# A hybrid mLSTM/GLA decoder block: the first two units side by side, with halved weight loads, constant products at the start and three squares on GpSimd

## The chip, the core and the metric

The kernel runs on one core of a Trainium2 chip. The core has a matrix engine (TensorE, PE in the profile), a vector engine (VectorE, DVE), an activation engine (ScalarE, ACT), a general engine (GpSimd, POOL) and a queue engine that issues DMAs (SyncE, SP). The engines run side by side, each takes its own instructions strictly in order, and they wait for each other by semaphores. The metric is the device time of one execution in microseconds (us); lower is better. Matmul results go to eight PSUM banks; everything else lies in SBUF.

## What is computed

The block takes 512 tokens of width 1024 and 16 learned meta tokens ahead of them, 528 in all. The part that matters here is its first step: a root-mean-square norm, and one wide projection of its result.

```python
def rmsnorm(x, g):
    xf = x.astype(jnp.float32)
    y = xf * lax.rsqrt(jnp.mean(xf * xf, axis=-1, keepdims=True) + EPS)
    return (y * g.astype(jnp.float32)).astype(x.dtype)
...
        xn = rmsnorm(h, norm1_g[l])
        proj = jnp.where(valid, xn @ w_in[l].astype(dt), 0.0).astype(dt)
        (mq, mk, mv, mi, mf, mo, gq, gk, gv, ga, gr, gate_m, gate_g) = split_cols(proj)
```

The columns of `proj` feed two token mixers (an mLSTM and a gated linear attention, both by chunks), whose results are merged by gates, projected and added to the input; a second norm and a SwiGLU follow, and a last norm. All of it is in float32.

## The kernel before

*Units.* All weights are cut into slices of 128 output columns. A slice is one unit: a tile of 128 partitions by 1024, whose eight blocks of 128 columns belong to the eight tiles of x. x lies transposed, as eight tiles `xs[k]` of 128 features by 528 tokens. The order of the units is fixed in `JOBS` (line 50 on): gates (0), mq (1), mk (2), two mv (3, 4), two mo (5, 6), then the next head, and so on.

*Products in three parts.* To keep float32 accuracy with the matrix engine's faster float32r format, every operand is split into a high part (a cast on ScalarE) and a low part (the rest, a subtraction on VectorE). `mm3` (line 297) adds three products for each tile of x: high weight by high x (line 302), high weight by low x (303), low weight by high x (304). The first units have 528 columns and need two banks, so a unit has 8 x 2 x 3 = 48 matmuls of 264 columns.

*Weights.* `load_raw` (177) puts a slice into one of four `raw` buffers through SP's queue. `split_hi` (188, ScalarE) and `split_lo` (193, VectorE) turn it into `whi` and `wlo`, four buffers each. When a split is issued is planned in `begin` (272): a list `ITEMS` of pending splits is worked off, one for each unit (tables `PLAIN`, `FIRST`, `SECOND` say after which tile of x each half of the step is issued). For single units `begin` plans one split further ahead than for pairs of units (`n += 1`), unless it is called with `more=False`.

*The start.* SP loads a block of parameters `pr`, the slice of unit 0, four tiles of x, the slice of unit 1, four more tiles, the slice of unit 2, and further constants (lines 417 to 450). ScalarE and VectorE split unit 0, then make for each tile of x a high part with the norm's gain (`act(..., scale=g)`, recorded at line 132) and a low part (line 471); after the sixth tile they split unit 1. Then ScalarE squares all eight tiles and VectorE adds the squares up into `xsum` (line 482), then unit 2 is split. TensorE runs unit 0 over all tiles of x and then unit 1 (`unit_all`, called at 1074 and 1075), then two plain float32 matmuls of `xsum` by a matrix of ones, which give the sum of squares over all features on every partition (line 1078). `rsqrt_mean` (490) turns it into the reciprocal root: a logarithm and an exponential on ScalarE (after a table load), then four steps on VectorE from line 496 on. The products of the first units are made from x without the norm; the root is multiplied in when a unit is taken out of PSUM (lines 593, 633, 716 and so on).

*Further on.* Generators (`run`, `mix`, `tick`) put the mixers' steps between the tiles of later units. During units 5 to 8 VectorE makes gate columns (line 683 and around), the normed x (508, 517) and the splits of coming units. `mlstm` begins with a cast of a selector on ScalarE (872) and two matmuls by it (875, 876).

GpSimd writes constants at the start, adds slices in memory by DMA for paired units (183, 212), and runs six elementwise products in the SwiGLU part (1294).

## Time and profile before

| | |
|---|---|
| median of 3 runs | 948.26 us (947.28 to 948.26) |
| the profiled execution | 948.52 us |
| its span, first to last instruction | 946.7 us |
| TensorE busy | 917.5 us |
| VectorE busy | 636.2 us |
| ScalarE busy | 546.2 us |
| GpSimd busy | 86.8 us |
| first matmul starts | 6.56 us |
| sum of squares starts | 22.23 us |

The profile is of one execution. The span leaves out 1.8 us around the instructions. A row of a timeline gives the start and the duration of an operation (or of x of them that follow each other), and in brackets how long the engine was idle before it and what released it. Matmuls overlap, so how fast TensorE goes is read from the distance between the starts of neighbouring matmuls and not from the duration of one. The releasers are inferred; a wait for several things is put down to the last.

### The profile page before, as it was taken

The page shows a single profiled execution, that of the slowest core. Times are in us where ns is not written, and L with a number is a line of the kernel's source. Part 1 is how long each engine was busy: PE and PEld are TensorE (multiplying, and loading weights), DVE is VectorE, ACT ScalarE, POOL GpSimd, SP SyncE. Part 2 cuts the span into 40 slices and gives each one's busy share as a digit, 9 for nine tenths or more (in the row PEclk, how much of TensorE's full clock was granted, in tenths as well). Part 3 has the DMA queues.
Part 4 walks back from the last instruction along what each step waited for, and adds up shares of the span by engine and source line. Part 5 has one row for each costly group of instructions (what it writes and reads, how often), then busy time and mean ns, then how long its engine had stood idle before and what let it go on. Part 6 is the DMA issues. An engine that isn't in the chain of part 4 may idle for free.

```text
span 946.7 us, 15478 instructions
## 1 busy us (share of the span) xinstructions
PE 917.5 (97%) x6083; PEld 842.3 (89%) x6083; DVE 636.2 (67%) x940; ACT 546.2 (58%) x954; POOL 86.8 (9%) x102
## 2 busy tenths in 40 slices
PE   6999999989999999999999999999999999999995
PEld 6988899878998899999998888888999999888885
DVE  6797776767875577777777556785767767842323
ACT  7557788779684256766874334443555555732321
POOL 0000022001100011110100000212121110000000
PEclk9999999989999999999999999999999999999998
DMA  7245375345562466655643343335788885322302
GB/s 262 101 139 155 119 162 123 75 112 134 127 163 90 111 148 155 163 120 141 134 134 107 116 133 116 107 102 132 185 186 179 189 191 148 115 94 85 111 1 89
DMA packets 48712, 124.45 MB, mean 131 GB/s; under 512 B 5376, under 2 KB 11520, under 8 KB 48640
## 3 DMA queue, kind: packets, MB, share of 16 engines
q1 hardware_dynamic: 35008, 101.32, 34.5%
q0 software_dynamic: 12544, 21.11, 14.5%
q8 instruction: 47, 0.77, 0.3%
q10 hardware_dynamic: 1088, 1.05, 0.3%
q14 instruction: 25, 0.20, 0.1%
HBM read 118.08 MB, written 5.37 MB: 130 GB/s over the span
## 4 chain that ended last, share of the span: by engine, by line
PE 78%; ACT 9%; DVE 8%; issue 3%; DMA 1%; DVEq 0%; SPq 0%; ACTq 0%
PE b L303 13%; PE b L302 13%; PE b L304 13%; PE b L344 12%; PE b L345 11%; PE b L346 11%; ACT t L132 4%; ACT whi L188 2%; DVE wlo L193 1%; ACT L130 1%; PE b L1056 1%; DVE t L716 1%; PE b L1058 1%; PE b L1035 1%; ACT L132 1%
## 5 line engine op out<-in xcount | busy, mean ns | idle before, releaser
L303 PE MATMUL b<-t,whi 128*128 128x512 f32 (+2 forms) x822 | 289.9, 353 | 1.0 <-DVE t L471 0.7
L302 PE MATMUL b<-t,whi 128*128 128x512 f32 (+2 forms) x774 | 274.0, 354 | 6.7 <-ACT t L132 6.6
L304 PE MATMUL b<-t,wlo 128*128 128x512 f32 (+2 forms) x774 | 270.8, 350 | 0.0
L344 PE MATMUL b<-t,whi 128*128 128x256 f32 (+1 forms) x864 | 250.0, 289 | 7.7 <-ACT t L404 6.1
L346 PE MATMUL b<-t,wlo 128*128 128x256 f32 (+1 forms) x864 | 245.1, 284 | 0.0
L345 PE MATMUL b<-t,whi 128*128 128x256 f32 (+1 forms) x864 | 245.0, 284 | 0.0
L193 DVE TENSOR_TENSOR wlo<-raw,whi 128x1024 fp32r<-128x1024 f32 x155 | 193.1, 1249 | 50.8 <-ACT whi L188 50.5
L188 ACT CAST whi<-raw 128x1024 fp32r<-128x1024 f32 x155 | 161.7, 1047 | 64.5 <-PE b L345 27.4
L303 PEld LDWEIGHTS b<-t,whi 128*128 128x128 f32 x822 | 155.8, 190 | 23.3 <-DVE t L843 1.1
L344 PEld LDWEIGHTS b<-t,whi 128*128 128x128 f32 x864 | 164.3, 190 | 9.9 <-ACT t L404 7.2
L302 PEld LDWEIGHTS b<-t,whi 128*128 128x128 f32 x774 | 147.0, 190 | 26.5 <-ACT t L132 6.6
L345 PEld LDWEIGHTS b<-t,whi 128*128 128x128 f32 x864 | 164.3, 190 | 0.5
L304 PEld LDWEIGHTS b<-t,wlo 128*128 128x128 f32 x774 | 146.8, 190 | 19.9 <-DVE wlo L193 0.3
L346 PEld LDWEIGHTS b<-t,wlo 128*128 128x128 f32 x864 | 164.0, 190 | 0.0
L132 ACT ACTIVATE t<-t 128x512 f32<-128x512 f32 (+6 forms) x124 | 70.4, 588 | 29.8 <-DVE t L1289 9.3
L183 POOL DMA_DIRECT2D raw<-wst x36 | 31.2, 867 | 364.4 <-DMA wf<-wst 104.9
L188 ACT CAST whi<-wf 128x1024 fp32r<-128x1024 f32 x36 | 37.8, 1051 | 22.5 <-PE b L345 13.5
L132 ACT ACTIVATE t<-f 128x256 f32<-128x256 f32 (+1 forms) x24 | 11.6, 482 | 61.6 <-DVE f L1456 61.6
L212 POOL DMA_DIRECT2D wf<-wst x36 | 32.5, 912 | 155.3 <-DMA wf<-wst 85.7
L193 DVE TENSOR_TENSOR wlo<-wf,whi 128x1024 fp32r<-128x1024 f32 x36 | 43.9, 1218 | 0.0
L1456 DVE TENSOR_TENSOR f<-f,b 128x512 f32<-128x512 f32 (+1 forms) x9 | 5.7, 629 | 53.3 <-PE b L304 53.3
L344 PE MATMUL b<-t,wgh 128*128 128x256 f32 (+1 forms) x144 | 41.0, 285 | 0.0
(219 smaller groups left out, 1216.6 us busy)
## 6 DMA issues: line engine op xcount, KB each, us to landing
raw<-wst SPq DMA_DIRECT2D x155, 512.0 KB, 3.6
wf<-wst SPq DMA_DIRECT2D x36, 256.0 KB, 3.2
wf<-wst POOLq DMA_DIRECT2D x36, 256.0 KB, 5.4
raw<-wst POOLq DMA_DIRECT2D x36, 256.0 KB, 4.7
t<-xT SPq DMA_DIRECT2D x8, 264.0 KB, 5.6
pos<-t SPq DMA_DIRECT2D x8, 264.0 KB, 2.3
t<-xT SPq DMA_DIRECT2D x8, 256.0 KB, 3.8
t<-neg POOLq DMA_DIRECT2D x6, 272.0 KB, 6.3
```

The costliest lines, as they stand in the source:

```text
L130: S.preload_act_table_set(want)
L132: S.activation(o, i, func, **kw)
L183: G.dma_start(lr(r, 0), lr(wst[v - 1], 0), accum_op=ALU.add)
L188: S.copy(t, src)
L193: V.tensor_tensor(t, src, hi.bitcast(F32), ALU.subtract)
L212: G.dma_start(lr(st.f, 1), lr(wst[u + 1], 1), accum_op=ALU.add)
L302: T.matmul(o, w_h, ah[:, c0:c1], start=first, stop=False)
L303: T.matmul(o, w_h, al[:, c0:c1], start=False, stop=False)
L304: T.matmul(o, w_l, ah[:, c0:c1], start=False, stop=last)
L344: T.matmul(o, h, xh_[k][:, c0:c1], start=start and k == 0, stop=False, skip_group_check=not start)
L345: T.matmul(o, h, xl_[k][:, c0:c1], start=False, stop=False, skip_group_check=not start)
L346: T.matmul(o, l, xh_[k][:, c0:c1], start=False, stop=k == 3, skip_group_check=not start)
```

## The change

The slices of units 0 and 1 are loaded and split in halves (`load_half`, `first_hi`, `first_lo`): the half for tiles 0 to 3 of x early, the other half after tile 4. `pr` goes through ScalarE's queue instead of SP's. A new function `first_units` runs units 0 and 1 together: for every tile of x, six matmuls of unit 0 and six of unit 1, in four banks. Ahead of them TensorE gets ten float32 matmuls of a matrix of ones by itself into a bank that nobody reads. The squares of tiles 0 to 2 and their two adds go to GpSimd; ScalarE squares the other five, VectorE adds these up and then GpSimd's sum. Since both calls of `begin` have `more=False`, the first two units issue one split instead of two, and all later ones are one unit later, until from unit 5 on `begin` may take a second split with the table `LATE`.

```diff
+    LATE = {"s": [(split_hi, 4), (split_lo, 6)]}
...
         if all(i[0] == "s" for i in ITEMS[n - 2:n + 1]) and len(names) == 1 and more:
             n += 1
+            if u > 4 and ready[0] < min(n, len(ITEMS)) - 1:
+                tables = [PLAIN, LATE]
...
+    def load_half(v, j):
+        if j == 0:
+            raws[v] = wpool.tile([P, D], F32, tag="raw", name=nm("raw"), bufs=4)
+            n_raw[0] += 1
+        nc.sync.dma_start(lr(raws[v], j), lr(wst[v], j))
...
+    S.dma_start(pr[:, :C_A2], par[:, :C_A2])
+    load_half(0, 0)
+    load_x()
+    load_half(1, 0)
+    for _ in range(4):
+        load_x()
+    load_half(0, 1)
+    load_half(1, 1)
+    for _ in range(3):
+        load_x()
     load_raw(2)
     nc.sync.dma_start(pr[:, C_A2:], par[:, C_A2:])
+
+    idle = bank()
+    for _ in range(10):
+        T.matmul(idle[:, :P], ones, ones, start=True, stop=True)
+    del idle
...
-        if k == 5:
-            split_hi(1)
-            split_lo(1)
-    xsum = tt()
-    for k in range(KT):
-        sq = xsum if k == 0 else tt()
-        act(sq, xs[k], AF.Square)
-        if k > 0:
-            V.tensor_tensor(xsum, xsum, sq, ALU.add)
...
+    for k in range(3):
+        sq[k] = tt()
+        G.tensor_tensor(sq[k], xs[k], xs[k], ALU.mult)
+        if k:
+            G.tensor_tensor(sq[0], sq[0], sq[k], ALU.add)
+            sq[k] = None
+    for f, v in ((first_hi, 0), (x_hi, None), (first_lo, 0), (first_hi, 1), (x_lo, None), (x_hi, None), (first_lo, 1),
+                 (x_lo, None), (x_hi, None), (x_lo, None), (x_hi, None), (x_lo, None)):
+        f() if v is None else f(v, 0)
+    x_hi()
+    x_lo()
+    for v in range(2):
+        first_hi(v, 1)
+        first_lo(v, 1)
+    for k in range(5, KT):
+        x_hi()
+        x_lo()
+    for k in range(3, KT):
+        sq[k] = tt()
+        act(sq[k], xs[k], AF.Square)
+    xsum = sq[3]
+    for k in range(4, KT):
+        V.tensor_tensor(xsum, xsum, sq[k], ALU.add)
+        sq[k] = None
     split_hi(2)
+    V.tensor_tensor(xsum, xsum, sq[0], ALU.add)
     split_lo(2)
...
-    ps_g = unit_all(("gates", 0))
-    ps_q = unit_all(("mq", 0))[0]
+    def first_units():
+
+        (u, s0), (v, s1) = begin(("gates", 0), more=False), begin(("mq", 0), more=False)
+        w = splits.pop(u), splits.pop(v)
+        ps = [[bank()[:, :HALF], bank()[:, :HALF]] for _ in range(2)]
+        for k in range(KT):
+            for o, ws in zip(ps, w):
+                for a in range(2):
+                    mm3(o[a], ws, k, X.h[k], X.l[k], a * HALF, (a + 1) * HALF, k == 0, k == KT - 1)
+            for q in (2 * k, 2 * k + 1):
+                for f in (s0, s1)[q // 8].get(q % 8, ()):
+                    f()
+        return (ps[0], None), ps[1]
```

The order of the instructions shows what becomes of it on the engines. VectorE at the start, before (`t` are tiles of x, their parts and the squares; lines 193 split weights, 471 make low parts of x, 482 add squares, 496 begins the root):

```order
L193 TENSOR_TENSOR wlo_148<-raw_81,whi_146 128x1024
L471 SCALAR_TENSOR_TENSOR t_152<-t_87,pr,t_150 128x528
L471 SCALAR_TENSOR_TENSOR t_156<-t_89,pr,t_154 128x528
L482 TENSOR_TENSOR t_158<-t_158,t_160 128x528
L482 TENSOR_TENSOR t_158<-t_158,t_163 128x528
L482 TENSOR_TENSOR t_158<-t_158,t_166 128x528
L482 TENSOR_TENSOR t_158<-t_158,t_169 128x528
L482 TENSOR_TENSOR t_158<-t_158,t_172 128x528
L482 TENSOR_TENSOR t_158<-t_158,t_175 128x528
L482 TENSOR_TENSOR t_158<-t_158,t_178 128x528
L193 TENSOR_TENSOR wlo_183<-raw_91,whi_181 128x1024
L193 TENSOR_TENSOR wlo_237<-raw_109,whi_223 128x1024
```

VectorE at the same place in the changed kernel (493 splits half a slice, 508 makes low parts, 534 and 537 add squares, 551 begins the root):

```order
L493 TENSOR_TENSOR wlo_146<-raw_77,whi_145 128x512
L508 SCALAR_TENSOR_TENSOR t_173<-t_89,pr,t_171 128x528
L508 SCALAR_TENSOR_TENSOR t_177<-t_91,pr,t_175 128x528
L508 SCALAR_TENSOR_TENSOR t_181<-t_93,pr,t_179 128x528
L534 TENSOR_TENSOR t_183<-t_183,t_185 128x528
L534 TENSOR_TENSOR t_183<-t_183,t_187 128x528
L534 TENSOR_TENSOR t_183<-t_183,t_189 128x528
L534 TENSOR_TENSOR t_183<-t_183,t_191 128x528
L537 TENSOR_TENSOR t_183<-t_183,t_131 128x528
L193 TENSOR_TENSOR wlo_200<-raw_95,whi_197 128x1024
L193 TENSOR_TENSOR wlo_312<-raw_122,whi_298 128x1024
L551 TENSOR_TENSOR t_331<-t_330 128x528
```

There are four half splits instead of two whole ones, five adds instead of seven, the last of them of GpSimd's sum, and two whole splits instead of three before the root.

GpSimd in the changed kernel, after its memsets (before, the DMA of line 212 follows the memsets directly):

```order
L514 TENSOR_TENSOR t_131<-t_75 128x528
L514 TENSOR_TENSOR t_133<-t_79 128x528
L516 TENSOR_TENSOR t_131<-t_131,t_133 128x528
L514 TENSOR_TENSOR t_136<-t_81 128x528
L516 TENSOR_TENSOR t_131<-t_131,t_136 128x528
L212 DMA wf_971<-wst 128x512
```

So five operations stand there that GpSimd did not have, and VectorE's line 537 waits for the last of them.

VectorE during unit 5, before (683 makes gate columns, 517 and 508 the normed x, 757 the low part of a transposed value tile):

```order
L683 TENSOR_SCALAR t_590<-t_482,t_481 32x128 x4
L193 TENSOR_TENSOR wlo_598<-raw_399,whi_578 128x1024
L683 TENSOR_SCALAR t_603<-t_590,t_481 32x128 x3
L517 TENSOR_TENSOR t_581<-t_568,t_580 128x528
L683 TENSOR_SCALAR t_614<-t_603,t_481 32x128 x2
L508 SCALAR_TENSOR_TENSOR t_623<-t_75,pr,t_317 128x528
L683 TENSOR_SCALAR t_633<-t_614,t_481 32x128
L757 TENSOR_TENSOR t_652<-b_628,t_640 128x512
L193 TENSOR_TENSOR wlo_657<-raw_469,whi_638 128x1024
```

and in the changed kernel, where the same steps have lines 738, 572, 563 and 812:

```order
L738 TENSOR_SCALAR t_603<-t_495,t_494 32x128 x4
L193 TENSOR_TENSOR wlo_611<-raw_343,whi_591 128x1024
L738 TENSOR_SCALAR t_618<-t_603,t_494 32x128 x3
L572 TENSOR_TENSOR t_594<-t_581,t_593 128x528
L193 TENSOR_TENSOR wlo_626<-raw_412,whi_613 128x1024
L738 TENSOR_SCALAR t_631<-t_618,t_494 32x128 x2
L563 SCALAR_TENSOR_TENSOR t_640<-t_79,pr,t_330 128x528
L738 TENSOR_SCALAR t_650<-t_631,t_494 32x128
L812 TENSOR_TENSOR t_669<-b_645,t_657 128x512
L193 TENSOR_TENSOR wlo_674<-raw_482,whi_655 128x1024
```

A second split of a whole slice has come in between the gate columns; everything behind it on VectorE moved back by one place.

## Rows read from the trace of the kernel before

**Rows 1.** Part 1 of the page: busy us (share of the span) x instructions.
```profile
PE 917.5 (97%) x6083; PEld 842.3 (89%) x6083; DVE 636.2 (67%) x940; ACT 546.2 (58%) x954; POOL 86.8 (9%) x102
```

**Rows 2.** Timeline of TensorE, 0 to 24: start, us, operation [idle before <-releaser].
```profile
6.56 0.59 PE L302 MATMUL b<-t,whi 128*128 128x264 f32 x1 [6.56 <-ACT t L132]
...
9.13 0.42 PE L302 MATMUL b<-t,whi 128*128 128x264 f32 x1
9.35 0.42 PE L303 MATMUL b<-t,whi 128*128 128x264 f32 x1
...
14.24 0.28 PE L302 MATMUL b<-t,whi 128*128 128x264 f32 x1
14.36 0.28 PE L303 MATMUL b<-t,whi 128*128 128x264 f32 x1
...
22.23 1.06 PE L1078 MATMUL b<-t,ones 128*128 128x264 f32 x4
22.93 0.48 PE L302 MATMUL b<-t,whi 128*128 128x264 f32 x1
```

**Rows 3.** Timeline of VectorE, 0 to 24.6 us.
```profile
5.91 1.23 DVE L193 TENSOR_TENSOR wlo<-raw,whi 128x1024 fp32r<-128x1024 f32 x1 [5.91 <-ACT whi L188]
7.05 2.80 DVE L471 SCALAR_TENSOR_TENSOR t<-t,pr,t 128x528 fp32r<-128x528 f32 x4
10.90 1.45 DVE L471 SCALAR_TENSOR_TENSOR t<-t,pr,t 128x528 fp32r<-128x528 f32 x2 [1.05 <-ACT t L132]
...
15.02 5.59 DVE L482 TENSOR_TENSOR t<-t,t 128x528 f32<-128x528 f32 x7
20.53 3.49 DVE L193 TENSOR_TENSOR wlo<-raw,whi 128x1024 fp32r<-128x1024 f32 x3
24.52 0.71 DVE L496 TENSOR_TENSOR t<-t 128x528 f32<-128x528 f32 x1 [0.50 <-ACT t L132]
```

**Rows 4.** Stretches: length; PE, PEld, DVE, ACT, POOL busy us; clock; DMA; GB/s.
```profile
4.00:5.00 1.00, 0.00 (x0) 0.00 (x0) 0.00 (x0) 0.17 (x1) 0.00 (x0) 1.00 1.00 389
44.00:67.00 23.00, 23.00 (x157) 20.61 (x156) 22.14 (x41) 10.87 (x17) 0.00 (x0) 1.00 0.38 125
198.00:200.00 2.00, 0.29 (x1) 0.29 (x2) 1.25 (x2) 1.99 (x5) 0.00 (x0) 0.58 0.79 123
...
204.00:206.00 2.00, 2.00 (x13) 2.00 (x13) 1.02 (x3) 0.38 (x1) 0.00 (x0) 0.71 0.00 0
```

**Rows 5.** Timeline of TensorE, at its wait for the selector cast.
```profile
69.60 0.50 PE L875 MATMUL b<-t,sel 128*128 128x512 f32 x1 [1.87 <-ACT sel L872]
```

**Rows 6.** Timeline of ScalarE, first cast, and the queue before the selector cast.
```profile
4.83 1.05 ACT L188 CAST whi<-raw 128x1024 fp32r<-128x1024 f32 x1 [2.81 <-DMA raw<-wst]
...
66.63 0.82 ACT L132 ACTIVATE t<-t,pr 128x512 f32<-128x512 f32 x1 [0.89 <-DVE t L593]
```

**Rows 7.** Timeline of GpSimd, 600 to 662 us, the first elementwise operations.
```profile
602.08 1.66 POOL L1294 TENSOR_TENSOR t<-t,t 128x512 f32<-128x512 f32 x1 [107.88 <-ACT t L132]
610.38 4.55 POOL L1294 TENSOR_TENSOR t<-t,t 128x512 f32<-128x512 f32 x1 [6.64 <-ACT t L132]
...
631.56 1.59 POOL L1294 TENSOR_TENSOR t<-t,t 128x512 f32<-128x512 f32 x1 [0.71 <-DVE t L1290]
```

**Rows 8.** Timeline of VectorE beside two of those.
```profile
613.86 1.62 DVE L1325 TENSOR_TENSOR t<-t,t 128x512 fp32r<-128x512 f32 x1
...
631.32 0.68 DVE L1325 TENSOR_TENSOR t<-t,t 128x512 fp32r<-128x512 f32 x1
631.92 2.32 DVE L193 TENSOR_TENSOR wlo<-raw,whi 128x1024 fp32r<-128x1024 f32 x1
```

**Rows 9.** TensorE's waits over the span: total us, times, longest us.
```profile
PE b L344 <- ACT t L404: 6.1, 4, 3.6
```

## What the change is predicted to do

> **What bounds the kernel now.** I read the page's totals first, then the first 25 us of each engine as a timeline, then the stretches in which an engine has no pause, and last TensorE's waits over the whole span. TensorE is busy 917.5 us, 97% of the span [rows 1], so no more than some 29 us can come from filling its gaps. Its longest wait stands at the front: 6.56 us before the first matmul, put down to the ScalarE activation that makes the first high part of x [rows 2]. [...] The two first units (96 matmuls) run from 6.56 to 22.23 us, where the sum of squares follows. At 0.12 us each they need 11.6 us. [...]
>
> What ends that stage is not TensorE alone. VectorE starts at 5.91 us and goes on to 24.02 us with little pause (eight low parts, seven adds of 0.80 us in a row, splits of weights at 1.16 us each when three follow each other), and takes up the reciprocal root of the mean (line 496) at 24.52 us [rows 3]. From there to 43 us the path goes to and fro between VectorE and ScalarE. From 44 to 67 us VectorE is busy 22.14 of 23 us [rows 4]: it is the bound there, and TensorE, which ran ahead, stops 1.87 us at 69.60 us [rows 5] for a selector cast that stands in ScalarE's queue behind a wait for VectorE [rows 6]. So what the change is worth is read at two places: **when line 496 can start, and whether VectorE's full stretch gets longer.** TensorE's own earlier start is worth only what VectorE can follow.
>
> **The change part by part.** *Loads.* The weights of units 0 and 1 come in halves. ScalarE's first cast waited until 4.83 us for a whole slice [rows 6]. Half a slice is 0.26 MB less, 0.7 us at the 389 GB/s of that time [rows 4], and the parameters are no longer ahead of it on SP. I take the first half cast at 4.0 us and VectorE's first split at 4.6 instead of 5.91 us. The parameters now delay ScalarE's first table load by one DMA issue; ScalarE idles 2.81 us there anyway [rows 6]. The last tile of x is ready 0.4 us earlier at most, since the bytes ahead of it are the same.
>
> *Constant products.* Ten matmuls of 128 columns in plain float32. [...] What they give back is clock, between nothing and the 4.1 us that the two units take now over their 11.6 us.
>
> *Two units side by side.* The same 96 matmuls, but each tile of x brings 12 of them (1.45 us fast, 2.64 us slow) instead of six, so TensorE has work while it waits for low parts that come every 0.70 us [rows 3]. With a fast clock and an undisturbed VectorE the two units end near 17.5 us and line 496 starts near 20.5 us, 4.0 us earlier; if the clock rises only at 11 us, 2.4 us earlier.
>
> *Squares on GpSimd.* Three squares leave ScalarE, which is not the bound. Two adds of 0.80 us leave VectorE. In exchange GpSimd runs five operations with two SBUF inputs. The trace has six of that kind, of 512 columns: 1.6 us each, one 4.55 us [rows 7]. **What they do to VectorE is the term that decides.** The one at 631.56 us left the VectorE row in progress at 0.68 us, until 632.00 us, and the next, a weight split, took 2.32 us [rows 8] where an undisturbed one takes 1.16 to 1.23 us. The long one ended after VectorE had paused, and a 0.68 us operation took 1.62 us [rows 7, 8]. So for about 1.1 us of each GpSimd operation VectorE stands still, and GpSimd stands still behind VectorE.
>
> [...] By the rows it is 1.1 to 1.15 us for each, since the first 0.45 us of the operation at 631.56 us held up nobody, and the sum goes by the rows.
>
> VectorE's sum up to line 496: four half splits at 0.6 us (2.4), eight low parts at 0.70 (5.6), five adds at 0.80 (4.0), two whole splits at 1.16 (2.3), together 14.3 us; now it is 17.0 us. To that come 5 x 1.15 = 5.75 us of standing still, of which some 0.4 us fall into pauses. From 4.6 us this ends at 24.3 us, with small waits between the first tiles at 24.7 us, against 24.52 us now: +0.2 us. Bounds of the standing still: nothing (all five in pauses) and 8 us (their whole duration). I take 5.75 us, since both stretched VectorE rows lie at 0.9 to 1.1 us.
>
> *One split fewer early, one more later.* The first two units make one split (unit 3) instead of two. Unit 4's goes back by a unit, and so on, until unit 5 makes two. So VectorE has 1.16 us less before line 496 (that is in the sum above) and 1.16 us more between the gate columns of unit 5. That place lies inside 44 to 67 us, where VectorE has no pause, and behind it are queued the rest of VectorE's work, ScalarE's line 132 at 66.63 us, which waits for VectorE, and so TensorE's wait at 69.60 us [rows 4 to 6]. ScalarE's extra cast is covered: it is busy 10.87 of 23 us there [rows 4]. Price of the split: 1.15 us, bound from below by 0 if a pause opens. Splits that move in the same way late in the program lie where VectorE has a third of its time free [rows 1]; I cost them at nothing.
>
> *Sum.* +0.2 us at line 496, +1.15 us at unit 5: **+1.35 us**. The profiled execution takes 948.52 us (946.7 us of span and 1.8 us around it), so it would take 949.9 us. The median of the runs is 0.26 us lower: 949.6 us.
>
> **The rivals.** *A: the front gain comes through*, because GpSimd falls into pauses of VectorE. For it: VectorE pauses 1.05 us between two low parts now [rows 3], and the first GpSimd operation can fall into such a gap. Against it: there are five operations and one such gap. Line 496 then starts 2.4 to 4.0 us earlier, by the clock; less 1.15 us at unit 5 that is 1.2 to 2.85 us off 948.26: 945.4 to 947.1 us, centre 946.2 us.
>
> *B: GpSimd's partial sum comes last* (slower). Its place is VectorE's add of sq[0], which stands in front of the sum of squares, and behind which the split for unit 2 is queued. GpSimd gets its turn only when VectorE pauses, as in the 4.55 us row [rows 7]. If one of the five is through when VectorE has done its four adds (about 17.0 us), four more of 1.6 us end near 23.5 us, the sum of squares starts at 23.9 instead of 22.23 us and line 496 at 26.1 us: +1.6 us, with unit 5 +2.75 us, 951.0 us. It decides as soon as the five take over 3.5 us each on average. The same time comes out if TensorE, starved by held-up low parts, stays at the slow level until 16 or 17 us: then the two units end near 23.5 us. The row for that: in its pause of 3.6 us at 196 us [rows 9] the granted clock fell to half, and it was back only between 204 and 206 us [rows 4]. [...]
>
> *C: the extra split of unit 5 finds a pause.* Then the sum is +0.2 us, 948.5 us, the forecast's low end.
>
> **How the numbers follow.** Forecast with C: 0.41. A: 0.31. B: 0.28. The forecast's own range is 948.3 to 950.9 us, from 1.0 to 1.3 us of standing still for each operation and 0 to 1.2 us for the split. 0.2% is 1.9 us, about what a measurement of this kernel can tell from no change: faster means under 946.4 us, slower over 950.2 us. Two thirds of A is faster (0.21), the rest within. A quarter of the forecast lies over 950.2 us (0.10), the rest within. B is slower but for a tenth. Together: faster 0.22, within 0.43, slower 0.35. Leaving out a tenth at each end cuts A at 945.9 us and B at 951.4 us.
>
> **What would show it.** Right: low parts or half splits that take 1.7 to 1.9 us beside GpSimd's squares, line 551 (line 496 of now) starting between 24 and 25.5 us, and TensorE waiting 3 us instead of 1.87 us for the selector cast. A shows in low parts all near 0.70 us and a sum of squares before 20 us. B shows in GpSimd's last add ending after VectorE's fourth, or in matmuls still 0.22 us apart after 14 us. The prediction is wrong in its ground if TensorE does not wait at the selector cast at all, since then VectorE is not what it follows, or if the waits for ScalarE's line 404 (6.1 us now [rows 9]) change by more than a microsecond.

## The result, and the profile after

The changed kernel takes **949.85 us** (median of 10 runs, 948.75 to 951.35), the kernel before 947.41 us beside it (10 runs): a ratio of 1.0026 with an interval of 1.0018 to 1.0033. It is slower by a quarter of a per cent. The forecast was 949.6 us, so the time was met. The difference behind it was not: the forecast added 1.35 us to 948.26 us, and the measured distance is 2.4 us from a kernel before that took 947.41 us this time. Its working did not hold either, and the rest of this text is on that.

The profiled execution took 950.18 us, with a span of 948.2 us, 1.5 us more than before (946.7 us). TensorE is busy 922.3 us, 97% of the span, as large a share as before [rows 1].

VectorE at the start, which answers to [rows 3] (start, duration, operation; lines 493 and 193 split weights, 508 makes low parts, 534 and 537 add squares, 551 begins the root):

```profile
4.56 0.69 DVE L493 TENSOR_TENSOR wlo<-raw,whi 128x512 fp32r<-128x512 f32 x1 [4.56 <-ACT whi L489]
5.40 1.34 DVE L508 SCALAR_TENSOR_TENSOR t<-t,pr,t 128x528 fp32r<-128x528 f32 x1
6.67 1.55 DVE L493 TENSOR_TENSOR wlo<-raw,whi 128x512 fp32r<-128x512 f32 x1
8.14 5.75 DVE L508 SCALAR_TENSOR_TENSOR t<-t,pr,t 128x528 fp32r<-128x528 f32 x4
...
17.05 3.13 DVE L534 TENSOR_TENSOR t<-t,t 128x528 f32<-128x528 f32 x4
20.29 0.71 DVE L537 TENSOR_TENSOR t<-t,t 128x528 f32<-128x528 f32 x1
20.92 2.35 DVE L193 TENSOR_TENSOR wlo<-raw,whi 128x1024 fp32r<-128x1024 f32 x2
23.45 0.71 DVE L551 TENSOR_TENSOR t<-t 128x528 f32<-128x528 f32 x1 [0.17 <-ACT t L132]
```

GpSimd in the same time, which answers to [rows 7]:

```profile
4.62 1.56 POOL L514 TENSOR_TENSOR t<-t 128x528 f32<-128x528 f32 x1 [2.81 <-DMA t<-xT]
6.54 1.13 POOL L514 TENSOR_TENSOR t<-t 128x528 f32<-128x528 f32 x1 [0.36 <-DMA t<-xT]
7.75 1.65 POOL L516 TENSOR_TENSOR t<-t,t 128x528 f32<-128x528 f32 x1
9.36 1.53 POOL L514 TENSOR_TENSOR t<-t 128x528 f32<-128x528 f32 x1
10.96 1.67 POOL L516 TENSOR_TENSOR t<-t,t 128x528 f32<-128x528 f32 x1
```

Three rows of VectorE are stretched, and all three lie beside GpSimd's five operations (4.62 to 12.63 us): one low part takes 1.34 us, a half split 1.55 us, four low parts 5.75 us. Behind 14 us everything has its usual size. GpSimd's operations go through although VectorE has hardly a pause there. The root starts at 23.45 us, **1.07 us earlier** than before (24.52 us [rows 3]).

TensorE, from the front to unit 7, answers to [rows 2, 5]:

```profile
6.80 0.39 PE L306 MATMUL b<-t,whi 128*128 128x264 f32 x1 [0.99 <-DVE t L508]
...
7.15 0.28 PE L305 MATMUL b<-t,whi 128*128 128x264 f32 x1
7.27 0.28 PE L306 MATMUL b<-t,whi 128*128 128x264 f32 x1
...
21.06 1.16 PE L1147 MATMUL b<-t,ones 128*128 128x264 f32 x4 [0.31 <-DVE t L537]
...
46.05 0.50 PE L307 MATMUL b<-t,wlo 128*128 128x512 f32 x1 [0.22 <-DVE wlo L193]
...
53.12 0.39 PE L305 MATMUL b<-t,whi 128*128 128x264 f32 x1 [1.26 <-ACT whi L188]
...
55.65 0.59 PE L307 MATMUL b<-t,wlo 128*128 128x264 f32 x1 [2.02 <-DVE wlo L193]
```

Neighbouring matmuls are 0.12 us apart from the start, where they were 0.22 us apart before, and they stay so through waits for low parts of 0.99 us at 6.80 us, 0.35 us at 8.27 us and 0.87 us at 10.02 us. The sum of squares (line 1147) waits for VectorE's last add. But there are three waits between 46 and 56 us, of 0.22, 1.26 and 2.02 us: for the low part of unit 6's weights, then for the high and the low part of unit 7's. They are new. The wait for the selector cast, 1.87 us at 69.60 us [rows 5], is gone, and so is one of 1.57 us that stood at 104 us before:

```profile
104.09 0.47 PE L939 MATMUL b<-wh,t 128*128 128x512 f32 x1 [1.57 <-DVE t L757]
```

In stretches (length; busy us of PE, PEld, DVE, ACT, POOL; granted clock; DMA; GB/s), the first answers to [rows 4]:

```profile
44.00:67.00 23.00, 19.50 (x112) 16.30 (x111) 22.22 (x41) 11.85 (x18) 0.00 (x0) 0.93 0.46 149
67.00:104.00 37.00, 37.00 (x252) 34.30 (x251) 28.45 (x51) 27.56 (x55) 1.91 (x2) 1.00 0.49 140
```

In 44 to 67 us TensorE is busy 19.50 us instead of 23.00, and its granted clock is 0.93 instead of 1.00. From 67 to 104 us it is busy without a pause: it has lost its reserve there. VectorE is as full as before, 22.22 of 23 us. The extra split of unit 5 and the first thing behind the gate columns (line 812, which is 757 of before):

```profile
54.39 1.21 DVE L193 TENSOR_TENSOR wlo<-raw,whi 128x1024 fp32r<-128x1024 f32 x1
...
56.73 1.21 DVE L193 TENSOR_TENSOR wlo<-raw,whi 128x1024 fp32r<-128x1024 f32 x1
...
59.13 0.67 DVE L812 TENSOR_TENSOR t<-b,t 128x512 fp32r<-128x512 f32 x1
```

The same two of the kernel before:

```profile
55.56 1.21 DVE L193 TENSOR_TENSOR wlo<-raw,whi 128x1024 fp32r<-128x1024 f32 x1
...
59.17 0.67 DVE L757 TENSOR_TENSOR t<-b,t 128x512 fp32r<-128x512 f32 x1
```

VectorE comes to the first of them 1.17 us ahead of the kernel before and to the second 0.04 us ahead. The second split, at 56.73 us, has taken 1.13 us. TensorE's waits for line 404, now 407, did not change (total, times, longest; before [rows 9]):

```profile
PE b L347 <- ACT t L407: 5.9, 4, 3.5
```

Up to 104 us the change is thus nearly neutral, and still the span is 1.5 us longer. The experiments look for the rest.

### The profile page after: what moved, and what is told of

The parts are those of the page before. It is cut to its first block, busy times and chain, and to the rows that moved or that the text cites. A ratio compares the mean times of both kernels' runs of the same rounds, so it can differ in the third digit from the quotient of the medians.

```text
span 948.2 us, 15521 instructions
## 1 busy us (share of the span) xinstructions
PE 922.3 (97%) x6103; PEld 846.0 (89%) x6103; DVE 640.1 (68%) x940; ACT 546.2 (58%) x953; POOL 94.3 (10%) x107
## 3 DMA queue, kind: packets, MB, share of 16 engines
q10 hardware_dynamic: 1232, 1.09, 0.3%
## 4 chain that ended last, share of the span: by engine, by line
PE 82%; ACT 8%; DVE 6%; issue 2%; DMA 1%; SPq 0%; DVEq 0%; ACTq 0%
PE b L305 14%; PE b L306 14%; PE b L307 14%; PE b L347 12%; PE b L348 11%; PE b L349 11%; ACT t L132 3%; ACT whi L188 1%; PE b L1111 1%; ACT L130 1%; PE b L1113 1%; PE b L1090 1%; ACT L132 1%; DVE wlo L193 1%; DMA t<-xT 1%
## 5 line engine op out<-in xcount | busy, mean ns | idle before, releaser
L193 DVE TENSOR_TENSOR wlo<-raw,whi 128x1024 fp32r<-128x1024 f32 x153 | 191.0, 1249 | 75.9 <-ACT whi L188 75.5
L188 ACT CAST whi<-raw 128x1024 fp32r<-128x1024 f32 x153 | 159.8, 1046 | 97.9 <-PE b L306 52.4
L347 PE MATMUL b<-t,wgh 128*128 128x256 f32 (+1 forms) x144 | 41.0, 285 | 0.0
L348 PE MATMUL b<-t,wgh 128*128 128x256 f32 (+1 forms) x144 | 40.8, 283 | 0.0
L349 PE MATMUL b<-t,wgl 128*128 128x256 f32 (+1 forms) x144 | 40.5, 281 | 0.0
```

The costliest lines, as they stand in the source:

```text
L188: S.copy(t, src)
L193: V.tensor_tensor(t, src, hi.bitcast(F32), ALU.subtract)
L347: T.matmul(o, h, xh_[k][:, c0:c1], start=start and k == 0, stop=False, skip_group_check=not start)
L348: T.matmul(o, h, xl_[k][:, c0:c1], start=False, stop=False, skip_group_check=not start)
L349: T.matmul(o, l, xh_[k][:, c0:c1], start=False, stop=k == 3, skip_group_check=not start)
```

## The experiments

The runs were timed in three groups, each group beside the kernel before on its chip. To see where time goes, the table takes one matmul at a time and asks how far behind the second trace of the kernel before (run b0) it starts, in us: the matmul is found in each trace by its number counted from the program's end. The head of a column is its time in b0. The last column is the time from VectorE's last instruction to the end of the span. At 85 us b0 itself is 1 us late, by its clock (0.95 from 67 to 104 us, with matmuls 0.22 us apart from 71.06 us on that were 0.12 us apart before; 1.00 in the first trace of the kernel before), so there most runs stand 1 us ahead of it.

| run | 23 | 46 | 60 | 85 | 104.5 | 190 | 206 | 655 | 917 | tail |
|---|---|---|---|---|---|---|---|---|---|---|
| before | +0.11 | +0.11 | +0.11 | -0.98 | +0.14 | +0.11 | +0.99 | +0.99 | +0.99 | 3.59 |
| changed | -0.96 | -0.77 | +5.04 | +1.60 | +0.24 | +0.28 | +1.26 | +1.21 | +2.12 | 3.97 |
| a0 | -1.02 | -0.82 | +5.03 | +1.58 | +0.19 | +0.22 | +0.21 | +0.13 | +1.04 | 3.97 |
| nopool | -2.41 | -2.38 | +5.31 | +1.71 | +0.29 | +0.28 | -0.02 | +0.21 | +0.30 | 4.08 |
| gap | -0.98 | -0.78 | -0.70 | -2.03 | -1.04 | -0.94 | -1.07 | -0.93 | -0.72 | 3.96 |
| early | -1.01 | -0.81 | -0.61 | -1.22 | -0.21 | -0.16 | -0.19 | -0.34 | +0.42 | 3.98 |
| noconst | -1.03 | -0.80 | +6.40 | +2.95 | +1.56 | +1.59 | +2.74 | +2.63 | +3.51 | 3.97 |
| np_gap | -2.62 | -2.59 | -2.59 | -2.41 | -2.41 | -2.41 | -2.63 | -2.42 | -2.25 | 4.07 |
| np_gap_seq | -1.13 | -1.09 | -1.09 | -2.25 | -1.14 | -1.11 | -0.33 | +0.15 | +0.45 | 4.08 |
| np_gap_tail | -1.93 | -1.90 | -1.90 | -2.81 | -1.72 | -1.74 | -3.27 | -3.08 | -2.90 | 3.86 |
| bconst | +0.04 | +0.04 | +0.04 | -1.04 | +0.04 | +0.05 | -0.19 | -0.25 | -0.24 | 3.59 |
| rot | -0.63 | -0.53 | -0.52 | -1.64 | -0.64 | -0.69 | -0.74 | -0.42 | -0.64 | 3.59 |

A row is one execution, and executions of one kernel differ. The one profiled of b0 took 947.53 us where the median of its runs is 947.22, of a0 948.88 (949.01), of gap 947.15 (947.92), of np_gap 945.73 (946.68), of np_gap_tail 944.87 (946.20). So the table says where time goes, to some tenths of a us, and the medians say what a kernel takes.

**b0 and a0: both kernels again, unchanged.**

> The kernel before, once more, to get its trace on the same chip as the others of this call. If the drift seen behind 104 us (the changed kernel's matmuls fell back by a further 0.9 us between 650 and 920 us, without a wait) belongs to a single execution or to the chip, this trace drifts against the first trace of before by some tenths of a us too, and the ratio is within 0.1% of 1. If it belongs to the change, this trace lies on the first one within 0.2 us everywhere.

> The changed kernel once more. Up to 104 us the same picture on either theory: root at 23.4 us, second split of unit 5 at 56.7 us, TensorE 0.1 to 0.3 us behind the kernel before at its line 939. If the rest of the loss belongs to the execution, TensorE is then still within 0.4 us of b0 at 917 us and the ratio is 1.000 to 1.001. If the change itself makes later stretches slower, TensorE is again 1 us behind at 917 us, and the ratio is again 1.002 to 1.003.

b0 took 947.22 us (ratio to the kernel before 1.0005, 0.9996 to 1.0013), a0 949.01 us (1.0027, 1.0016 to 1.0038). The loss is the kernel's, not an execution's. The table shows two things. Two executions of one kernel differ by steps (so the 0.2 us everywhere that was expected of b0 did not come), at places where TensorE's clock falls: before against b0 by 0.9 us between 190 and 206 us, the changed kernel against a0 by 1.0 us at the same place. There the granted clock over 196 to 207 us was 0.69 in the changed kernel's trace (first row) and 0.84 in a0's:

```profile
196.00:207.00 11.00, 7.47 (x37) 7.00 (x36) 4.97 (x8) 7.66 (x17) 0.86 (x1) 0.69 0.55 120
```

```profile
196.00:207.00 11.00, 7.45 (x45) 7.04 (x45) 6.04 (x8) 8.70 (x19) 0.86 (x1) 0.84 0.59 121
```

Behind that they lie on each other: before against b0 stays at +0.99 from 206 to 917 us. Between the two kernels there is a slow drift instead, and it repeats: a0 goes from +0.21 to +1.04 us, the changed kernel from +1.26 to +2.12 us. Here are line 939 (now 994) and a matmul near the end in b0 and then in a0; the distance grows from 0.27 to 1.02 us, and no wait stands for it:

```profile
103.95 0.48 PE L939 MATMUL b<-wh,t 128*128 128x512 f32 x1 [1.19 <-DVE t L757]
...
936.23 0.70 PE L1482 MATMUL b<-t,ones 128*128 128x256 f32 x2 [0.96 <-ACT t L132]
```

```profile
104.22 0.39 PE L994 MATMUL b<-wh,t 128*128 128x512 f32 x1
...
937.25 0.70 PE L1551 MATMUL b<-t,ones 128*128 128x256 f32 x2 [0.96 <-ACT t L132]
```

The theory that the drift belongs to an execution or a chip has fallen.

**nopool: the squares back on ScalarE, their adds back on VectorE.**

```diff
-    for k in range(3):
-        sq[k] = tt()
-        G.tensor_tensor(sq[k], xs[k], xs[k], ALU.mult)
...
-    for k in range(3, KT):
+    for k in range(KT):
...
-    V.tensor_tensor(xsum, xsum, sq[0], ALU.add)
```

> The changed kernel with the three squares back on ScalarE and their adds back on VectorE; all else as changed. Theory: GpSimd's five operations hold VectorE up for about 4.5 us and save it two adds (1.6 us), and VectorE's row sets the start of the root. Then the low parts take 0.70 us each, the root starts at 21 us (23.45 us with GpSimd), VectorE and TensorE stay some 2 us ahead up to 104 us, and the run takes 2 us less than the changed kernel. Rival: TensorE's 96 matmuls, which ended at 20.5 us, set the sum of squares and not VectorE; then they start with the first operands as before, the root starts at 22.9 us or later, and the run gains 0.5 us or less.

948.36 us, ratio 1.0012 (1.0003 to 1.0021). VectorE, the four low parts that took 5.75 us, and the root:

```profile
7.42 2.90 DVE L508 SCALAR_TENSOR_TENSOR t<-t,pr,t 128x528 fp32r<-128x528 f32 x4 [0.47 <-ACT t L132]
...
22.20 0.71 DVE L544 TENSOR_TENSOR t<-t 128x528 f32<-128x528 f32 x1 [0.37 <-ACT t L132]
```

Four low parts take 2.90 us. With the other two stretched rows (0.77 and 0.69 us here) GpSimd held VectorE up for 0.57 + 0.86 + 2.85 = 4.3 us (4.1 us by a0's rows). The root came 1.25 us earlier than in the changed kernel, not the 2.4 us that was expected: two adds are back (1.7 us), and VectorE now pauses 1.5 us in all for ScalarE. At 104 us nothing was left of that. TensorE waits for the weights of units 6 and 7 as in the changed kernel, and its clock falls behind these waits, for longer than in a0 (granted clock over 56 to 67 us):

```profile
56.00:67.00 11.00, 11.00 (x63) 9.80 (x62) 9.79 (x18) 6.44 (x10) 0.00 (x0) 0.69 0.68 233
```

```profile
56.00:67.00 11.00, 11.00 (x75) 9.99 (x74) 10.48 (x19) 6.00 (x10) 0.00 (x0) 0.84 0.68 228
```

So it is 5.3 us behind b0 at 60 us and has no reserve left at 104 us. VectorE had been made faster and TensorE had become the bound. In the runs nopool takes 0.65 us less than a0, not the 2 us that were expected, and these do not come from the front: at 104.5 us it stands 0.1 us behind a0, and what it gains on a0's trace comes behind 206 us, where it drifts by 0.3 instead of 0.8 us. The next run has TensorE as the bound for its rival; here that holds.

**gap: the extra split in VectorE's pause.**

```diff
+        if 2 <= u <= 5:
+            steps = {}
+            for f, v, at in {2: ((split_hi, 4, 2), (split_lo, 4, 4), (split_hi, 5, 5)), 3: ((split_hi, 6, 2), (split_lo, 5, 4)),
+                             4: ((split_lo, 6, 3), (split_hi, 7, 2), (split_lo, 7, 4)),
+                             5: ((split_hi, 8, 2), (split_lo, 8, 4))}[u]:
+                steps.setdefault(at, []).append(lambda f=f, v=v: f(v))
```

> The changed kernel with its GpSimd squares, but with the extra split in another place: one cast is moved from unit 5 to unit 2, where ScalarE waits 3.3 us, and one low part of a split from unit 5 to the 3.1 us in which VectorE waits for ScalarE at 39 to 42 us. Theory: the extra split of unit 5 costs VectorE 1.15 us in a stretch without pause, and it is what TensorE waits for at 53 and 55.7 us. Then VectorE is 1.1 us ahead of the kernel before from 59 us on, TensorE does not wait for weights there but at the selector cast as before, and the run takes 1.0 to 1.2 us less than the changed kernel. Rival: TensorE is bound by its own work from 56 to 147 us (it had no wait there), so the earlier splits only move its waits to the selector cast and to the line that waited 1.57 us before, and the run gains 0.3 us or less.

947.92 us, ratio 1.0014 (1.0005 to 1.0023), 1.1 us less than a0 in the same group. VectorE does the split where it waited 3.14 us for ScalarE, and the wait that is left is 1.90 us:

```profile
39.15 1.23 DVE L193 TENSOR_TENSOR wlo<-raw,whi 128x1024 fp32r<-128x1024 f32 x1
42.27 0.70 DVE L710 TENSOR_TENSOR t<-t,t 32x528 f32<-32x528 f32 x1 [1.90 <-ACT t L132]
```

TensorE waits for no weights; its two waits of before are back:

```profile
PE b L1000 <- DVE t L818: 1.6, 1, 1.6
PE b L936 <- ACT sel L933: 1.5, 1, 1.5
```

In the table TensorE is 0.7 us ahead at 60 us and 1.04 us ahead at 104.5 us, where a0 was 5.0 and 0.2 us behind. The lead of 1 us that the front gained comes through to there. To the end it does not: the median lies 0.7 us above that of the kernel before, although this trace's span is 0.3 us shorter than b0's; the execution traced is the second fastest of eleven.

**early: two splits ahead of the root again.**

```diff
-        (u, s0), (v, s1) = begin(("gates", 0), more=False), begin(("mq", 0), more=False)
+        (u, s0), (v, s1) = begin(("gates", 0)), begin(("mq", 0))
```

> The changed kernel with GpSimd's squares, but the first two units issue two splits again, as before the change, so that nothing is one unit later and no second split stands in unit 5. Theory: VectorE has 1.16 us more ahead of the root, which then starts at 24.6 us as before the change (24.5); from there on VectorE lies within 0.2 us of the kernel before; TensorE does not wait for the weights of units 6 and 7, and stands 0 to 0.2 us behind the kernel before at 104 us. The end is that plus the tail (0.4 us) and a drift of either sign up to 0.8 us: ratio 1.000 to 1.0015. Rival: the loss behind unit 7 has nothing to do with the later splits; then TensorE is again 3 us or more behind the kernel before at 60 us.

948.64 us, ratio 1.0016 (1.0007 to 1.0025), a little over the expected 1.0015. VectorE has three splits in a row again and starts the root at 24.28 us:

```profile
20.87 3.49 DVE L193 TENSOR_TENSOR wlo<-raw,whi 128x1024 fp32r<-128x1024 f32 x3
24.28 0.70 DVE L551 TENSOR_TENSOR t<-t 128x528 f32<-128x528 f32 x1
```

TensorE has no wait for weights and is 0.6 us ahead at 60 us: with the splits where they were, the 5 us of a0 are gone, so they come from the splits being one unit later. At 104.5 us that is worth only 0.4 us, since a0 catches up where b0 waits. The root, with a third split ahead of it, starts 0.9 us later than a0's 23.38 us. From 104.5 us (-0.21) the run loses 0.6 us by drift and 0.4 us by its tail.

**noconst and bconst: the constant products, taken away and alone.**

```diff
-    idle = bank()
-    for _ in range(10):
-        T.matmul(idle[:, :P], ones, ones, start=True, stop=True)
-    del idle
```

(noconst, on the changed kernel; bconst puts the same four lines into the kernel before.)

> The changed kernel without the ten constant products. Theory: they pay by the clock alone. Without them TensorE starts at 5.4 us as with them, its neighbouring matmuls are 0.22 us apart until about 12 us, and the some 27 matmuls that it has done by then take 2.7 us longer, of which 2.0 us fall into its waits for low parts: sum of squares 0.4 to 1.0 us later than 21.06 us, root the same amount later, 104 us and the end within 0.5 us, since TensorE is the bound behind unit 7 there. Rival: the clock costs the front its full 2.7 us or more, and the run takes over 1.5 us longer than the changed kernel. Of the slow drift behind 206 us: its x tiles lie in memory as in the changed kernel, its PSUM banks as in the kernel before; a drift of 0.8 us against b0 from 206 to 917 us speaks for the tiles, none for the banks.

> The kernel before with nothing but the ten constant products ahead of its first unit. Theory: VectorE is the bound of the front. Matmuls are 0.12 us apart from the first one on, TensorE ends its two units 1.0 to 1.4 us earlier, the root starts 0.3 to 0.5 us earlier (VectorE's third split ends at 24.02 us), and 104 us and the end are 0.2 to 0.5 us earlier. Rival: TensorE is the bound of the front, then the root starts 1.2 us earlier and the run gains 1 us or more. Of the slow drift: its tiles lie in memory as in the kernel before and its PSUM banks in part in others; a drift over 0.3 us against b0 from 206 to 917 us speaks for the banks.

noconst took 950.4 us (1.0032, 1.0019 to 1.0044), bconst 947.29 us (1.0001, 0.9992 to 1.001). In noconst the matmuls are 0.22 us apart at 7 us (7.33, 7.55, 7.77 us), and the root still starts where it did:

```profile
23.38 0.71 DVE L547 TENSOR_TENSOR t<-t 128x528 f32<-128x528 f32 x1 [0.17 <-ACT t L132]
```

The sum of squares starts at 21.08 us, in the changed kernel at 21.06 us. Expected were 0.4 to 1.0 us more for both. So the shorter steps that the constant products give at the front, 0.12 instead of 0.22 us, are worth nothing to the root of this kernel, since VectorE's last add, held up by GpSimd, is just as late; np_gap, where it is not, was not run without them. Nor was it expected that there would be 1.4 us more loss between 46 and 104 us: behind the waits for weights the granted clock over 56 to 67 us is 0.69 here and was 0.84 in a0, as in nopool. How long the clock stays down differs between executions of one kernel at 196 us too (0.69 and 0.84 over 196 to 207 us), so one execution doesn't show that the missing products are the cause; that stays open, and noconst's interval (five runs) overlaps a0's. In bconst TensorE is starved after its constant products: it waits 1.56 us for its first operand, does one matmul, waits 0.91 us for a low part at 8.05 us, and behind that its matmuls are 0.22 us apart again (granted clock 0.57 from 8 to 12 us); the root starts at 24.45 us, in b0 at 24.41 us:

```profile
6.75 0.39 PE L302 MATMUL b<-t,whi 128*128 128x264 f32 x1 [1.56 <-ACT t L132]
8.05 0.59 PE L303 MATMUL b<-t,whi 128*128 128x264 f32 x1 [0.91 <-DVE t L475]
...
8.66 0.42 PE L302 MATMUL b<-t,whi 128*128 128x264 f32 x1
8.88 0.42 PE L303 MATMUL b<-t,whi 128*128 128x264 f32 x1
```

Both expectations of a gain there failed.

**np_gap and np_gap_seq: both cures together, and side by side undone.** np_gap is nopool and gap together. np_gap_seq takes it and runs unit 0 before unit 1:

```diff
-        for k in range(KT):
-            for o, ws in zip(ps, w):
+        for o, ws, s in zip(ps, w, (s0, s1)):
+            for k in range(KT):
```

> The changed kernel without GpSimd's squares and with the extra split in VectorE's gap at 37 to 41 us. Theory: VectorE sets the path from the root to 104 us, and TensorE only follows once it does not wait for the weights of units 6 and 7. Then the root starts at 22.2 us as in the run without GpSimd's squares, VectorE is 2.3 us ahead of the kernel before from there to 128 us, TensorE too at its line 939 of the kernel before, and the end is 1.5 to 2.3 us ahead of it (ratio 0.9976 to 0.999). Rival: TensorE's own work or its clock is the bound behind 60 us; then it is no further ahead at 104 us than the run with the moved split alone, 1.0 us.

> The run without GpSimd's squares and with the moved split, but units 0 and 1 one after the other again, halves and constant products kept. Theory: VectorE sets the root, and side by side is worth only what keeps TensorE from being later than VectorE's sum: unit 0 goes at the pace of the low parts to 13.7 us, unit 1 takes 5.9 us at the fast clock, the sum of squares starts at 19.7 to 20.5 us instead of 19.4, the root 0.3 to 1.0 us later, and 104 us and the end as much later. Rival: TensorE starves in unit 0, its clock falls as it did at 8 us with the constant products alone, and the sum of squares starts at 21.5 us or later; then side by side is worth 2 us, nearly all of the front's gain.

np_gap took 946.68 us (0.9991, 0.9982 to 1.0), np_gap_seq 947.69 us (1.0008, 0.9999 to 1.0017). np_gap's ratio lies just above the 0.9976 to 0.999 that were expected. In np_gap TensorE is 2.6 us ahead at 23 us and still 2.41 us ahead at 104.5 us: VectorE sets the path, and TensorE follows. One after the other, the root starts at 23.27 instead of 21.99 us, first np_gap, then np_gap_seq:

```profile
21.99 0.71 DVE L550 TENSOR_TENSOR t<-t 128x528 f32<-128x528 f32 x1 [0.38 <-ACT t L132]
```

```profile
23.27 0.71 DVE L550 TENSOR_TENSOR t<-t 128x528 f32<-128x528 f32 x1 [0.96 <-ACT t L132]
```

TensorE's clock tells the two apart from 5 to 12 us, in the same order:

```profile
5.00:12.00 7.00, 6.66 (x49) 6.21 (x49) 6.37 (x10) 6.36 (x11) 0.00 (x0) 1.00 1.03 389
```

```profile
5.00:12.00 7.00, 5.70 (x27) 4.92 (x27) 5.83 (x9) 5.72 (x10) 0.00 (x0) 0.79 1.02 378
```

But a load came later in this execution, too: ScalarE's second half cast, at 5.35 us in np_gap without a wait, starts at 6.24 us here, and VectorE's adds end 0.7 us later. np_gap_tail, which has its units side by side and the same load late (at 6.54 us), has its matmuls 0.12 us apart between its waits up to 12 us and starts its root at 22.67 us; first np_gap_seq's cast, then that root:

```profile
6.24 0.62 ACT L495 CAST whi<-raw 128x512 fp32r<-128x512 f32 x1 [0.88 <-DMA raw<-wst]
```

```profile
22.67 0.71 DVE L555 TENSOR_TENSOR t<-t 128x528 f32<-128x528 f32 x1 [0.37 <-ACT t L132]
```

So side by side is worth between 0.6 us (against np_gap_tail) and 1.3 us at the root, which does not contradict the theory's 0.3 to 1.0 us. The clock fell to 0.79 in this stretch as the rival had it, but the sum of squares starts at 21.00 us, between the theory's 20.5 and the rival's 21.5 us.

**rot: the kernel before with its tiles in other places.**

```diff
+    spare = tt()
+    G.memset(spare, 0.0)
+    del spare
```

> The kernel before with one tile of the size of a tile of x taken, zeroed by GpSimd at the start and given back, so that later tiles lie in other places of SBUF (31% of the matmuls read their x side from another place); the work is the same. Theory: the steps between matmuls depend by some nanoseconds on where their operands lie, and the changed kernel's loss behind 206 us is of that kind. Then this kernel drifts against b0 by 0.2 to 0.8 us, to either side, between 206 and 917 us, with the same waits. Rival: the drift comes from the changed work (splits that come later, other loads); then there is none here, and the steps agree to within 1 ns as they do between two executions of the kernel before.

947.57 us, ratio 1.0001 (0.9992 to 1.001). Against b0 it goes from -0.74 us at 206 us to -0.35 us at 600 us and back to -0.64 us at 917 us: a swing of 0.4 us, but 0.1 us from end to end, less than the 0.2 us that were expected. Nothing was added but one memset at the start, so the places alone make steps of some tenths of a us. The single distances between neighbouring matmuls behind 206 us show it more plainly: against b0, 50% of them differ by more than 2 ns in rot and 49% in a0, but 3% in the other trace of the kernel before and 4% in bconst. Noconst has its tiles where the changed kernel has them and its banks where the kernel before has them, and it drifts by 0.77 us; bconst has it the other way round and drifts by 0.05 us. **The PSUM banks are not the reason, and the places of the tiles in SBUF are for a good part.** Noconst shares not only its tiles' places but its work with the changed kernel, so the rival that the drift comes from the changed work needs other runs. From 67 us on, TensorE, VectorE and ScalarE do the same work in the same order in early, gap, nopool, np_gap and np_gap_tail as in a0, with tiles in other places, and drift by 0.61, 0.35, 0.32, 0.38 and 0.37 us instead of 0.83 us. So some 0.5 us of the 0.83 us are not the work's. All five do drift forward, though, and whether the remaining 0.3 us belong to the late splits, whose order differs from that of the kernel before up to 920 us, no run separates. Which property of a place does it stays open too.

**np_gap_tail: six small loads.**

```diff
+    for i in range(6):
+        nc.sync.dma_start(full[:, NT + i:NT + i + 1], par[:, i:i + 1])
```

> The run without GpSimd's squares and with the moved split, plus six loads of one column each into unused columns of a tile of x, which nobody reads. Theory: the changed kernel and its offspring take 0.37 us longer than the kernel before between VectorE's last instruction and the end of the span (3.97 to 4.08 us against 3.59 us), because the number of DMAs shifted by two: the eight DMA semaphores are used in turn, SyncE checks them in a fixed order at the end, 0.06 us each, and now six stand behind the one of the last landing. Six more DMAs turn that back: the tail is 3.6 to 3.7 us, the rest of the trace lies on that of the run without them within 0.2 us up to 190 us, and the time is 0.4 us less: ratio 0.9978 to 0.9995. Rival: the tail belongs to the output's landing, then it stays at 4.0 us.

946.2 us, **ratio 0.9986 (0.9977 to 0.9994)**: the one run whose whole interval lies below 1. VectorE's last row in b0 and SyncE's last steps there, then in a0 (of the line's groups: count, durations in ns, first and last start):

```profile
939.63 2.50 DVE L1495 TENSOR_TENSOR t<-t,t 128x512 f32<-128x512 f32 x4
```

```profile
L1604 SPq DRAIN  x3: 7/7/7, 944.9 to 945.2; - x3
```

```profile
940.64 2.50 DVE L1564 TENSOR_TENSOR t<-t,t 128x512 f32<-128x512 f32 x4
```

```profile
L1673 SPq DRAIN  x3: 7/7/7, 946.3 to 946.6; - x3
```

VectorE ends at 942.13 and 943.14 us, SyncE drains from 944.9 and 946.3 us on: 2.8 and 3.1 us later. The records of landings and of SyncE's waits tell why. In b0 SyncE drains 0.08 us after the last output has landed, in a0 and np_gap 0.44 us after it, with six checks of 0.06 us between; in np_gap_tail it is 0.08 us again. That part of the tail is shown. The tail as a whole went only from 4.07 to 3.86 us and not to the expected 3.6 to 3.7 us, because in this execution the last landing itself came 0.26 us later. Nor does the trace lie on np_gap's up to 190 us as expected: from the late load at the front on it is 0.7 us behind it. Between 190 and 206 us it gains 1.3 us on np_gap; that is the clock, which did not fall there in this execution (1.00 over 196 to 207 us, 0.84 in np_gap), and is an execution's, not the loads'.

## Why the prediction held, and where it was wrong

- **The front (+0.2 us forecast, -1.07 us measured).** The start was right: the first half split at 4.6 us forecast and 4.56 us measured. The term that failed is GpSimd's: 5 x 1.15 = 5.75 us of standing still, plus 0.4 us of small waits. The changed trace and nopool show 4.3 us, 0.86 us for each operation, with hardly a pause. With 4.3 in place of 5.75 us the forecast's 24.7 us become 23.25 us, and the last split of that sum ended at 23.27 us. The rows of the kernel before gave the mechanism, and the price from two of them was a third too high. The forecast's upper bound, the whole duration of all five, would make it 7.5 us by the recorded durations; the traces show 4.3 us. Whether a recorded duration holds a wait of GpSimd's own, the trace does not show. One reading was off too: VectorE's sum is not the whole path to the root. Before the change VectorE stood idle 0.50 us ahead of the root [rows 3], which waited, by way of ScalarE, for the sum of squares behind TensorE's two units; in the changed kernel VectorE's last add sets the sum of squares, and the root comes 0.17 us behind the splits. Early, with its third split back, starts the root at 24.28 us: 0.8 to 0.9 of the 1.07 us are that split's.
- **The extra split of unit 5 (+1.15 us forecast, 1.13 us measured).** Right in place and size, on VectorE; gap, which takes it away, stands 1.2 us further ahead at 104.5 us. The two terms together would have been +0.1 us.
- **Where TensorE waits.** The forecast said 3 us at the selector cast. There is no wait there at all, and by the forecast's own words its ground was then wrong. What it left out is that the moved splits are not only VectorE's work but the weights that TensorE is about to need. Units 6 and 7 got theirs one unit later, and TensorE, 0.8 us ahead, ran into them: 3.5 us of waits, then a slow clock (0.84 over 56 to 67 us in a0, 1.00 in b0), 5.0 us behind at 60 us. Its reserve was what it waited before, 1.87 and 1.57 us and some shorter stops; it used all of that, and 0.2 us remained at 104 us. The run early shows it by undoing that one step. Of the three signs that the forecast named for being right none came: the stretched rows take 1.34 to 1.55 us (1.7 to 1.9), the root starts at 23.45 us (24 to 25.5), and the cast is not waited for.
- **Behind 104 us (nothing forecast, 1.2 us measured).** 0.8 us of drift and 0.4 us of tail (SyncE's six checks) in a0. The tail and most of the drift are in no sum of work; the late splits, which the forecast costed at nothing, can have up to 0.3 us of it (see rot). So the forecast of +1.35 us met +1.4 us of span (a0 against b0) by luck, by two errors of about the same size: a front that was 1.3 us too slow, and an end that was 1.2 us too fast. The medians lie 1.8 us (a0's group) to 2.4 us (the result) apart, 0.4 to 1.0 us more than these spans. In a0's group that is where the two traced executions lie: b0's 0.3 us above its median, a0's 0.1 us below. What more there is in the result, the traces don't settle; single executions differ by 0.9 to 1.5 us between 190 and 206 us, where the granted clock over 196 to 207 us is 0.69 (before), 0.84 (b0) or 1.00 (np_gap_tail).
- **The rivals.** A, that the front's gain comes through, was half right: 1.07 us came, from one split less and little else, not from pauses, and its signs (low parts near 0.70 us, a sum of squares before 20 us) did not come. B's place was wrong: GpSimd's last add ended at 12.63 us, long before VectorE's fourth add at 20.2 us; it did not need VectorE's pauses. Its five operations took 1.13 to 1.67 us each and not over 3.5 us; the first took 1.56 us, behind 2.81 us of idle time that the profile puts down to a load. C would have been gap's picture: the split in a pause, 1.1 us back. (A small slip in the chances: two thirds of A's 0.31 are 0.21, where the total says 0.22.)

## What to carry to other kernels

When work is moved to a later step, two prices are to be asked for: the time of the engine that does it, and the lead of the engine that needs its result. A wait that TensorE has at the end of a stretch is a reserve, and a change that spends it shows no loss there until it is gone, so count it before moving its operands. And a part that frees a bound by 1.4 us (nopool against a0 at 23 us) can have nothing left of it at 104 us until the next bound is freed too (np_gap against gap, still 1.4 us): test such parts together as well as alone.

## What was not expected of the hardware

- Steps between matmuls depend on where the tiles lie in SBUF: with one tile shifted (rot) half of them differ by more than 2 ns from b0's (3% in another execution of the kernel before), and their sum swings by 0.4 us. Between the two kernels of this text the sum is 0.8 us over 700 us, in two executions of each, for a good part by the places.
- One wait of TensorE of 3.6 us at 196 us has a different sequel in different executions of the same kernel: granted clock 0.69 or 0.84 over the 11 us around it, 0.9 to 1.0 us of time.
- GpSimd's operations with SBUF inputs held VectorE up for 4.3 us in all, of 7.5 us that they took (1.13 to 1.67 us each): 0.86 us each on average.
- Two more DMAs at the start cost 0.36 us at the end, by the order in which SyncE checks eight semaphores, 0.06 us each: in the first trace of the kernel before the last output lands on the eighth of them and SyncE drains 0.08 us later, in the changed kernel's it lands on the second and SyncE drains 0.45 us later.
- The steps of 0.12 us that constant products give (0.22 us in noconst) can be lost again before the real work: bconst's matmuls were 0.22 us apart, at a granted clock of 0.57 from 8 to 12 us, behind waits of 1.56 and 0.91 us with one matmul between them, while the changed kernel's stayed 0.12 us apart through waits of 0.99, 0.35 and 0.87 us.
